# Twenty small copies per layer of a two-block transformer kernel, from VectorE to ScalarE

## The chip, the cores and the metric

The kernel runs on one core of a Trainium2 chip. What counts is the device time of one execution in microseconds (us). Its engines are TensorE (PE, with its weight loads listed as PEld), VectorE (DVE), ScalarE (ACT), GpSimd (POOL) and SyncE (SP), which issues nearly all DMAs. Each engine takes its instructions in the order in which they stand in its own queue and waits on semaphores for the others.

## The reference, cut to what matters

The reference chains two blocks of two layers each on a sequence of 512 tokens of width 1024, all in float32. The change lies in the second block, in the attention of each of its two layers:

```
def nsa_mixer(q, k_all, v_all, gates, q_norm, k_norm, cmp_pe, cmp_w1, cmp_w2):
    q = rope(rms_norm(q, q_norm), pos)                  # 8 heads of 64
    k_s = rope(rms_norm(k_all[:, :, 1], k_norm[1]), pos)  # 2 groups
    k_w = rope(rms_norm(k_all[:, :, 2], k_norm[2]), pos)
    k_cmp = rope(rms_norm(compress(k_all[:, :, 0], ...), k_norm[0]), cmp_end)  # 31 keys
    v_cmp = compress(v_all[:, :, 0], ...)
    o_cmp = softmax(q k_cmp) v_cmp;  o_s = softmax(q k_s) v_s;  o_w = softmax(q k_w) v_w
    return g[..., 0] * o_cmp + g[..., 1] * o_s + g[..., 2] * o_w
```

Around it stand a projection of the layer's input (pooling inputs, keys and values, queries, gates), a pooling mixer, an output projection and a feed-forward network.

## The kernel before

**Arithmetic.** A float32 product is made of three matmuls in the type fp32r: a value is split into a high half (a cast to fp32r) and a low half (the value minus the high half), and high times high, high times low and low times high are summed. Weights come in units of 128x1024 by DMA (`wraw`) and are cut by `unit`: the high half `wH` by a cast on ACT (line 452), the low half `wL` by a subtraction on DVE (line 453). Activations are mostly cut by `split`: a cast on ACT (419), a subtraction on DVE (420).

**The stage of the change.** In `block2`, `weave` interleaves four generators: `main2` makes the projections (their accumulators are `acc` and `accn`), `nsa_prep` and then `nsa` the attention, `compressed` the 31 compressed keys, `pool` the pooling mixer. `nsa_prep` takes the four 128-token tiles of the queries, one after the other: sums of squares (588, 590), the root by a power on POOL (578), the rotation (1573 and 1577 on DVE, 1576 on POOL), the high half (1621) and the low half (1622) of a 128x512 tile `qs`, eight transposes on PE by a product with the identity `keep` (415), and two casts on ACT into `qT` (1628). The keys go the same way in four 128x256 tiles (1639 to 1651), with a copy of the high half on POOL (1643). `compressed` ends with the halves of 64x64 compressed keys (1673 to 1675), and eight copies of 32x128 pieces of the compressed values into `vc` (1694).

`nsa` then runs 16 steps, 8 heads by 2 branches. A step is a chain over the engines: scores on PE (tiles `S`), mask, scale and row maximum on DVE (710), the exponential on ACT (711), the division by the sum on POOL (1764) and DVE (1766), transposes on PE (415, tiles `M`), a split (419 on ACT, 420 on DVE), and the product with the values on PE (406, `M<-p,b`). `main2` puts the last matmuls of the pooling projection and the output projection (`accn`, added up on DVE by 1507) between them.

**Order.** The functions write the program in the order of `weave`; then the Tile framework's scheduler, at build time, orders each engine's queue by its own estimate of when each instruction can run. So an instruction moved from one engine to another can change the order of others, far behind it, too.

## Time and profile before

| | |
|---|---|
| median of 3 runs | 2393.4 us (2393.25 to 2394.74) |
| the profiled execution | 2391.33 us, span of its instructions 2389.5 us |
| PE, DVE, ACT, POOL busy | 98%, 69%, 44%, 11% of the span |
| attention stage of layer 1 of block 2 | about 1240 to 1420 us of the span |
| the same of layer 2 | about 1840 to 2010 us |

A row of the page's list of groups gives a line, an engine, an operation, its tiles and count, then the busy time and the mean of one, then how long the engine had been idle just before and what ended that. A row of the timeline gives the start, the duration, and in square brackets the idle time before it. PE's rows overlap each other, as matmuls are pipelined: the distance from start to start is what one costs.

### The profile page before, as it was taken

Reading aid. Unit: us, or ns where it says so; the run is one execution under the profiler, and the core shown is the slowest. Engines: PE = TensorE matmul, PEld = TensorE weight load, DVE = VectorE, ACT = ScalarE, POOL = GpSimd, SP = SyncE. Lnnn points to the kernel's source line nnn. Section 1 sums busy time; section 2 is a strip of 40 time slices with the busy share of each in tenths; the row PEclk is TensorE's granted clock in tenths of the full one; section 3 lists DMA queues with packets and bytes.
Section 4 is the critical chain, followed back from the end, with each engine's and each line's share of the span. In section 5 each row is a group of like instructions: output and inputs, shape, how many; then the busy total and the mean of one; then the engine's idle time right before and its main releaser. Section 6 shows DMA issues by size and latency. Waiting matters only on the chain.

```text
span 2389.5 us, 31476 instructions
## 1 busy us (share of the span) xinstructions
PE 2342.3 (98%) x11684; PEld 1973.3 (83%) x11684; DVE 1640.2 (69%) x3410; ACT 1048.7 (44%) x1930; POOL 264.3 (11%) x254
## 2 busy tenths in 40 slices
PE   8999999999999999999999989999999998999999
PEld 7888888888888888888888778888888876888888
DVE  5679975567588987656579886666647988644342
ACT  6455543434446554343246654332324665433231
POOL 0011010000001001000055310000005531000000
PEclk9999999999999999999999999999999999999999
DMA  5222222245543222225332013555523211223222
GB/s 173 88 80 71 80 80 97 82 156 205 182 159 115 71 80 80 97 88 172 126 102 80 27 37 104 193 194 194 193 97 105 68 35 37 80 94 100 98 93 84
DMA packets 87851, 256.62 MB, mean 107 GB/s; under 512 B 9745, under 2 KB 10769, under 8 KB 87697
## 3 DMA queue, kind: packets, MB, share of 16 engines
q1 hardware_dynamic: 87552, 254.45, 31.9%
q8 instruction: 92, 1.51, 0.3%
q14 instruction: 63, 0.51, 0.1%
q10 hardware_dynamic: 144, 0.15, 0.0%
HBM read 250.37 MB, written 4.19 MB: 107 GB/s over the span
## 4 chain that ended last, share of the span: by engine, by line
PE 93%; DVE 5%; ACT 1%; issue 1%; DMA 0%; POOL 0%; DVEq 0%; ACTq 0%; POOLq 0%
PE acc L406 78%; PE M L406 5%; PE accn L406 4%; PE S L406 3%; PE M L415 3%; DVE p L420 1%; DVE p L710 1%; DVE b L1507 1%; DVE wL L453 1%; ACT p L419 0%; DVE p L1766 0%; ACT p L711 0%; DVE tmp_s L1794 0%; DMA wraw<-wp_in 0%; ACT tmp_s L1792 0%
## 5 line engine op out<-in xcount | busy, mean ns | idle before, releaser
L406 PE MATMUL acc<-h,wH 128*128 128x512 f32 (+2 forms) x2944 | 872.6, 380 | 9.5 <-ACT h L423 7.3
L452 ACT CAST wH<-wraw 128x1024 fp32r<-128x1024 f32 x358 | 375.2, 1051 | 656.8 <-PE acc L406 400.0
L406 PEld LDWEIGHTS acc<-h,wH 128*128 128x128 f32 (+1 forms) x2944 | 537.4, 189 | 106.1 <-ACT h L423 7.3
L453 DVE TENSOR_TENSOR wL<-wraw,wH 128x1024 fp32r<-128x1024 f32 x358 | 437.5, 1223 | 164.9 <-ACT wH L452 156.9
L406 PE MATMUL acc<-h,wL 128*128 128x512 f32 (+1 forms) x1440 | 546.2, 380 | 0.0
L406 PE MATMUL acc<-b,wH 128*128 128x512 f32 (+1 forms) x1696 | 503.9, 374 | 0.0
L406 PEld LDWEIGHTS acc<-b,wH 128*128 128x128 f32 x1696 | 311.8, 189 | 56.3
L406 PEld LDWEIGHTS acc<-h,wL 128*128 128x128 f32 x1440 | 272.7, 190 | 49.6
L406 PE MATMUL acc<-wH,h 128*128 128x512 f32 (+1 forms) x1024 | 310.0, 380 | 0.0
L406 PE MATMUL acc<-b,wL 128*128 128x512 f32 (+1 forms) x784 | 291.5, 372 | 0.0
L406 PEld LDWEIGHTS acc<-wH,h 128*128 128x128 f32 x1024 | 187.2, 188 | 33.7
L406 PE MATMUL acc<-wL,h 128*128 128x512 f32 (+1 forms) x512 | 194.7, 380 | 0.0
L1390 DVE SCALAR_TENSOR_TENSOR b<-acc,keep,b 128x512 f32<-128x512 f32 (+1 forms) x68 | 48.9, 720 | 183.9 <-PE acc L406 183.5
L406 PEld LDWEIGHTS acc<-b,wL 128*128 128x128 f32 x784 | 147.9, 189 | 25.4
L711 ACT ACTIVATE p<-p,nb 128x128 f32<-128x128 f32 x192 | 107.9, 564 | 77.7 <-DVE nb L710 76.7
L1325 DVE SCALAR_TENSOR_TENSOR keep<-keep 128x512 f32<-128x512 f32 x192 | 126.0, 686 | 11.1 <-DMA keep<-w_mod_in 10.9
L578 POOL TENSOR_TENSOR sm_bs<-sm_as,keep 128x4 f32<-128x4 f32 (+1 forms) x48 | 65.7, 1376 | 413.4 <-DVE sm_as L574 374.1
L406 PEld LDWEIGHTS acc<-wL,h 128*128 128x128 f32 x512 | 96.5, 188 | 16.2
L406 PE MATMUL S<-b,b 128*128 128x128 f32 (+3 forms) x480 | 108.9, 338 | 0.1
L710 DVE CUSTOM_DVE_ANT_0 p<-S,keep 128x128 f32<-128x128 f32 x192 | 101.3, 542 | 4.9 <-PE S L406 3.6
L415 PE MATMUL M<-keep,p 128*128 128x128 f32 x608 | 97.4, 275 | 2.7 <-DVE tmp_s L1794 1.0
L406 PE MATMUL M<-p,b 128*128 128x256 f32 (+3 forms) x352 | 81.7, 323 | 10.3 <-DVE p L420 9.0
(294 smaller groups left out, 2898.8 us busy)
## 6 DMA issues: line engine op xcount, KB each, us to landing
wraw<-wp_in SPq DMA_DIRECT2D x364, 512.0 KB, 3.5
keep<-w_mod_in SPq DMA_DIRECT2D x192, 256.0 KB, 3.6
b<-x_in SPq DMA_DIRECT2D x8, 256.0 KB, 6.3
g<-x_in SPq DMA_DIRECT2D x8, 256.0 KB, 4.4
x_spill<-tmp_m SPq DMA_DIRECT2D x8, 256.0 KB, 3.9
g<-x_spill SPq DMA_DIRECT2D x8, 256.0 KB, 3.8
out<-b SPq DMA_DIRECT2D x6, 256.0 KB, 2.0
keep<-parq_in SPq DMA_DIRECT2D x2, 384.0 KB, 6.9
```

The costliest lines, as they stand in the source:

```text
L406: return self.nc.tensor.matmul(out, l, r, start=start, stop=stop)
L415: self.nc.tensor.transpose(out, in_, self.ident[:n, :n])
L420: return self.nc.vector.tensor_sub(l, src, fbits(h))
L452: self.cut_h = nc.scalar.copy(h, raw)
L453: self.cut = nc.vector.tensor_sub(l, raw, fbits(h))
L578: self.pow = nc.gpsimd.tensor_tensor(r[:p, :n], m[:p, :n], self.mhalf[:p, :n], ALU.pow)
L710: nc.vector.tensor_tensor_reduce(p, s, mask, nscale, 3e38, ALU.add, ALU.min, accum_out=nb)
L711: nc.scalar.activation(p, p, AF.Exp, bias=nb, scale=-1.0, accum_out=accum)
L1325: nc.vector.scalar_tensor_tensor(w, w, 1.0, crow[:, T * k:T * k + T], ALU.mult, ALU.mult, accum_out=ms[:, 2 * f + k:2 * f + k + 1])
L1390: nc.vector.scalar_tensor_tensor(x(m)[:, ts], ps[:, ts], mt[:, 40 + m:41 + m], x(m)[:, ts], ALU.mult, ALU.add)
L1507: nc.vector.scalar_tensor_tensor(x(m)[:, ts], ps[:, ts], mt[:, 16 + m:17 + m], x(m)[:, ts], ALU.mult, ALU.add)
```

## The change

Five lines, in `nsa_prep` and `compressed`, say `nc.scalar.copy` in place of `nc.vector.tensor_copy`. Per layer these are 4 casts of 128x512 (queries), 4 casts of 128x256 (keys), a cast and a copy of 64x64 (compressed keys), and 8 copies of 32x128 (compressed values). All else of the text is the same.

```
-            nc.vector.tensor_copy(qs[:, :, 0, :].bitcast(F32R), qr)
+            nc.scalar.copy(qs[:, :, 0, :].bitcast(F32R), qr)
             nc.vector.tensor_sub(qs[:, :, 1, :], qr, qs[:, :, 0, :])
...
-            nc.vector.tensor_copy(ks[:, :, 0, :].bitcast(F32R), kn)
+            nc.scalar.copy(ks[:, :, 0, :].bitcast(F32R), kn)
             nc.vector.tensor_sub(ks[:, :, 1, :], kn, ks[:, :, 0, :])
             nc.gpsimd.tensor_copy(ks[:, :, 2, :], ks[:, :, 0, :])
...
-        nc.vector.tensor_copy(ks[:, 0, :].bitcast(F32R), kc[:, 2, :])
+        nc.scalar.copy(ks[:, 0, :].bitcast(F32R), kc[:, 2, :])
         nc.vector.tensor_sub(ks[:, 1, :], kc[:, 2, :], ks[:, 0, :])
-        nc.vector.tensor_copy(ks[:, 2, :], ks[:, 0, :])
+        nc.scalar.copy(ks[:, 2, :], ks[:, 0, :])
...
-                nc.vector.tensor_copy(vc[32 * h:32 * h + 32, g, h, :], fbits(vs[32 * g:32 * g + 32]).rearrange("p w d -> p (w d)"))
+                nc.scalar.copy(vc[32 * h:32 * h + 32, g, h, :], fbits(vs[32 * g:32 * g + 32]).rearrange("p w d -> p (w d)"))
```

The queues change at more places than these. On ACT, at the queries of layer 1 (`p_2073` and `p_2083` are the tiles `qs` of the first and the second 128 tokens, `tmp_s_2071` and `tmp_s_2081` the rotated queries):

```order
 L588 ACTIVATE tmp_s_2077_10906<-b_2062_10848 128x512
 L1466 COPY b_2062_10848<-acc_2048_10726 128x512
+L1621 CAST p_2073_10881<-tmp_s_2071_10875 128x8x64
 L588 ACTIVATE tmp_s_2094_10973<-b_2062_10848 128x512
 L452 CAST wH_2118_11079<-wraw_11077 128x1024
 L1466 COPY b_2062_10848<-acc_2049_10727 128x512
+L1621 CAST p_2083_10921<-tmp_s_2081_10915 128x8x64
 L588 ACTIVATE tmp_s_2120_11107<-b_2062_10848 128x512
```

Two casts now stand between the squares of later tiles, a weight cast and an eviction of projected queries.

On PE, at the same place (`M_2075` and `M_2076` take the transposes of the first tile of queries, `acc_2085` is a sum of the key and value projection):

```order
 L406 MATMUL acc_2085_10927<-wH_2090_10933,h_1986_10307 128x512
 L406 MATMUL acc_2085_10927<-wH_2090_10933,h_1985_10306 128x512
+L415 MATMUL M_2075_10894<-keep_1_61,p_2073_10881 128x128 x4
+L415 MATMUL M_2076_10900<-keep_1_61,p_2073_10881 128x128 x4
 L406 MATMUL acc_2085_10927<-wL_2091_10934,h_1985_10306 128x512
 L406 MATMUL acc_2085_10927<-wH_2090_10933,h_1986_10307 128x512
```

These eight transposes stood 14 projection matmuls later before.

On PE, at the first scores of the attention (`M_2173` and `M_2174` take transposes of the third tile of keys, `S_2187` and `S_2189` are the first scores of head 0, `accn_2207` a sum of the pooling projection):

```order
+L415 MATMUL M_2173_11335<-keep_1_61,p_2172_11331 128x128
 L406 MATMUL accn_2207_11446<-h_1985_10306,wH_2205_11442 128x512
 L406 MATMUL accn_2207_11446<-h_1986_10307,wH_2205_11442 128x512
-L415 MATMUL M_2173_11335<-keep_1_61,p_2172_11331 128x128 x4
+L406 MATMUL accn_2207_11446<-h_1985_10306,wL_2206_11443 128x512
+L415 MATMUL M_2173_11335<-keep_1_61,p_2172_11331 128x128 x3
 L415 MATMUL M_2174_11341<-keep_1_61,p_2172_11331 128x128 x4
 L406 MATMUL S_2187_11381<-b_2146_11252,b_2065_10864 128x128 x2
-L406 MATMUL accn_2207_11446<-h_1985_10306,wL_2206_11443 128x512
 L406 MATMUL accn_2207_11446<-h_1987_10308,wH_2205_11442 128x512
```

One projection matmul went from behind the first score to ahead of it.

On PE, in the middle of the attention (`S_2364` and `S_2367` are scores of head 3 against the selected keys, `S_2376`, `S_2382` and `S_2390` scores of head 3 against the window's keys, `M_2344` the last product of the pooling mixer):

```order
 L406 MATMUL S_2364_12060<-b_2146_11252,b_2065_10864 128x384 x2
 L406 MATMUL S_2367_12071<-b_2146_11252,b_2065_10864 128x512 x2
-L406 MATMUL S_2376_12105<-b_2147_11253,b_2065_10864 128x128 x2
-L406 MATMUL S_2382_12121<-b_2147_11253,b_2065_10864 128x256 x2
-L406 MATMUL S_2390_12167<-b_2147_11253,b_2065_10864 128x384 x2
 L406 MATMUL M_2344_11973<-tmp_p_2339_11959,b_2199_11425 128x512
 L406 MATMUL M_2346_11986<-p_2327_11917,b_2139_11197 128x512
```

The three scores taken out here now stand further back, one at a time between transposes and products with the values. Layer 2 has the same differences at the same places. SP's queue is the same in both.

## Rows read from the trace of the kernel before

**Rows 1.** The page: busy time by engine, and the chain that ended last.

```profile
PE 2342.3 (98%) x11684; PEld 1973.3 (83%) x11684; DVE 1640.2 (69%) x3410; ACT 1048.7 (44%) x1930; POOL 264.3 (11%) x254
PE 93%; DVE 5%; ACT 1%; issue 1%; DMA 0%; POOL 0%; DVEq 0%; ACTq 0%; POOLq 0%
```

**Rows 2.** Stretch, length, busy us (count) of PE, PEld, DVE, ACT, POOL, clock, DMA.

```profile
1245.00:1300.00 55.00, 55.00 (x288) 46.11 (x287) 49.84 (x128) 30.57 (x71) 32.66 (x35) 1.00 0.29 96
1300.00:1420.00 120.00, 109.15 (x613) 89.30 (x612) 105.89 (x291) 76.94 (x209) 37.37 (x44) 1.00 0.11 36
...
1845.00:1900.00 55.00, 55.00 (x292) 46.24 (x291) 48.60 (x133) 32.39 (x77) 29.08 (x36) 1.00 0.22 70
1900.00:2010.00 110.00, 101.25 (x569) 82.82 (x568) 99.35 (x272) 71.40 (x195) 33.47 (x39) 1.00 0.10 34
```

**Rows 3.** PE's waits, 1300 to 1420: total us, times, longest.

```profile
PE M L406 <- DVE p L420: 4.5, 9, 1.0
PE accn L406 <- ACT b L419: 2.0, 1, 2.0
```

**Rows 4.** Groups of VectorE by shape, 1240 to 1300: busy us, mean ns.

```profile
L1621 DVE CAST p<-tmp_s 128x512 fp32r<-128x512 f32 x4 | 2.1, 533 | 0.1
...
L1694 DVE CAST b<-tmp_c 32x128 fp32r<-32x128 f32 x8 | 1.7, 218 | 0.2
...
L1673 DVE CAST tmp_c<-tmp_c 64x64 fp32r<-64x64 f32 x1 | 1.7, 1651 | 0.0
...
L1641 DVE CAST p<-tmp_s 128x256 fp32r<-128x256 f32 x4 | 1.4, 351 | 0.0
```

**Rows 5.** Groups of ScalarE by shape, 1230 to 1300: casts out of SBUF.

```profile
L419 ACT CAST tmp_p<-tmp_p 128x512 fp32r<-128x512 f32 x1 | 0.6, 623 | 0.0
...
L419 ACT CAST tmp_c<-tmp_c 64x64 fp32r<-64x64 f32 x1 | 0.2, 244 | 1.1 <-POOL sm_bc L578 1.1
```

**Rows 6.** Timeline of VectorE at the queries of layer 1: start, us, instruction.

```profile
1242.78 1.12 DVE L1577 TENSOR_TENSOR tmp_s<-tmp_s,tmp_s 128x512 f32<-128x512 f32 x1
...
1244.49 0.41 DVE L1621 CAST p<-tmp_s 128x512 fp32r<-128x512 f32 x1
1244.82 0.68 DVE L1577 TENSOR_TENSOR tmp_s<-tmp_s,tmp_s 128x512 f32<-128x512 f32 x1
...
1246.78 1.13 DVE L1622 TENSOR_TENSOR p<-tmp_s,p 128x512 f32<-128x512 f32 x1
...
1248.18 1.21 DVE L453 TENSOR_TENSOR wL<-wraw,wH 128x1024 fp32r<-128x1024 f32 x1
...
1251.26 0.68 DVE L1622 TENSOR_TENSOR p<-tmp_s,p 128x512 f32<-128x512 f32 x1
```

**Rows 7.** Timeline of ScalarE there: the weight cast behind the first moved cast.

```profile
1243.63 1.05 ACT L452 CAST wH<-wraw 128x1024 fp32r<-128x1024 f32 x1 [1.20 <-DMA wraw<-wp_in]
```

**Rows 8.** The chain that ended last, 1240 to 1300: start, us, what.

```profile
1248.77 0.87 PE M L415 x8
1249.64 2.74 PE acc L406 x12
```

**Rows 9.** Timeline of GpSimd at the same place.

```profile
1245.66 1.70 POOL L1576 TENSOR_TENSOR tmp_s<-b,keep 128x256 f32<-128x256 f32 x2
...
1251.22 1.82 POOL L1576 TENSOR_TENSOR tmp_s<-b,keep 128x256 f32<-128x256 f32 x2
```

**Rows 10.** Timeline of VectorE at the first scores of layer 1 and layer 2.

```profile
1290.63 0.62 DVE L710 CUSTOM_DVE_ANT_0 p<-S,keep 128x384 f32<-128x384 f32 x1 [1.66 <-PE S L406]
...
1884.23 0.62 DVE L710 CUSTOM_DVE_ANT_0 p<-S,keep 128x384 f32<-128x384 f32 x1 [1.98 <-PE S L406]
```

**Rows 11.** Timeline of TensorE in mid-attention, then VectorE a little later.

```profile
1330.74 2.97 PE L406 MATMUL S<-b,b 128*128 128x128 f32 x14
1335.53 0.50 PE L406 MATMUL M<-tmp_p,b 128*128 128x512 f32 x1 [1.83 <-ACT tmp_p L419]
...
1348.05 0.75 DVE L1507 SCALAR_TENSOR_TENSOR b<-accn,keep,b 128x512 f32<-128x512 f32 x1 [1.97 <-PE accn L406]
```

## The prediction

> **What bounds the kernel now.** I read the page's busy times and its chain first: TensorE is busy 98% of the span, and 93% of the chain that ended last is its own work [rows 1]. So a move between VectorE and ScalarE can change the time only where TensorE waits. Next, the table of stretches [rows 2]. From 1245 to 1300 us, where all twenty copies of layer 1 lie, TensorE is busy 55.00 of 55.00 us; layer 2 reads the same from 1845 to 1900. VectorE has 49.84 of these 55 us, ScalarE 30.57. In the attention behind it, from 1300 to 1420, TensorE has 109.15 of 120 us, so 10.85 us are idle, and in layer 2 (1900 to 2010) 110 - 101.25 = 8.75 us. These 19.6 us are all that the attention of both layers could give back. Third, TensorE's waits in that stretch [rows 3]: the largest is for the low half of the transposed probabilities on VectorE (4.5 us in 9 waits), next 2.0 us for a ScalarE cast. VectorE's load, 105.89 of 120 us, is the nearest rival of TensorE there, and none of the moved copies lies in it.
>
> **What leaves VectorE.** Per layer, from the groups by shape [rows 4]: four casts of 128x512 for 2.1 us, four of 128x256 for 1.4 us, one of 64x64 for 1.65 us, eight of 32x128 for 1.7 us, and the 64x64 copy, counted like one of the eight, 0.2 us. The sum is 7.0 us, and 49.84 would become about 43.
>
> **What comes to ScalarE.** The nearest rows are casts from SBUF to SBUF: 623 ns for 512 columns, 244 ns for 64 [rows 5], so 0.846 ns a column; an estimate from these is 406 ns for 256 and 298 ns for 128. Four by 623, four by 406, two by 244 and eight by 298 make 2.49 + 1.62 + 0.49 + 2.38 = 7.0 us. ScalarE goes from 30.57 to about 37.6 of 55 us. What hides this is its 24 us of idle time; without it the 7.0 us would stand once per layer before the attention.
>
> **The waits that are added.** A cast that followed its input on VectorE now takes a turn to ScalarE and back. I follow the first tile of queries. Its rotated values were ready when the 1.12 us addition ended, at 1243.90 [rows 6]. On ScalarE the cast takes 0.62 us, to about 1244.5. What is queued behind it there (squares of a later tile, then a weight cast) slips: that weight cast started at 1243.63 [rows 7] and would start at about 1243.90 + 0.62 + 0.6 = 1245.1. The subtraction that needs it ran only at 1248.18 [rows 6], more than two microseconds after the new end of 1246.2. So that costs nothing. On VectorE the subtraction 1622 now waits for ScalarE, with sums and rotations of later tiles behind it; the order puts the second tile's addition ahead of it as a filler: 1244.49 + 0.68 = 1245.17, later than the cast's end, so VectorE should not stand still.
>
> TensorE is another matter. The eight transposes of that tile started at 1248.77, and the order lifts them past 14 matmuls of 2.74/12 = 0.228 us [rows 8], 3.2 us, so to 1245.6. Their input is ready when the low half is: 1245.17 plus 0.68 to 1.13 us, the two durations that line 1622 shows [rows 6], so 1245.85 to 1246.30. TensorE waits 0.25 to 0.7 us where it did not wait before; I take 0.5. The ends for the range are 0 (the transposes come just in time) and 1.2 (the hand-over to ScalarE finds the engine busy with one more 0.6 us operation).
>
> The long subtraction started at 1246.78, while GpSimd was at work from 1245.66 to 1247.36; but the short one, at 1251.26, had GpSimd beside it too, from 1251.22 [rows 9]. So the rows do not settle which length the new one has, and 0.5 stays the middle.
>
> The Trainium skill (GPSIMD Engine Reference, Specifications) says that GpSimd shares its SBUF interfaces with VectorE and contends with VectorE instructions that have two SBUF inputs, as this subtraction has. By that rule the new subtraction, at 1245.2 beside GpSimd's work, would take 1.13 us and TensorE's wait be 0.7, the sum 0.4 us higher over both layers; this trace agrees at the one place and not at the other.
>
> The later tiles have more room. Their transposes move by 0 to 1.4 us of TensorE's work, counted in the order by columns at that pace, while VectorE reaches their subtractions earlier by what has left it. The compressed keys' chain gets shorter (0.24 in place of 1.65 us for its cast). The keys' copy on GpSimd now waits for ScalarE instead of VectorE and still has the freed time as cover. I set all these at nothing; without the cover each would cost one hand-over of the size above, 0.5 us.
>
> **Where the 7 us on VectorE go.** At the first scores VectorE already waits: it stood idle 1.66 us before 1290.63 in layer 1 and 1.98 us before 1884.23 in layer 2, both times for scores from TensorE [rows 10]. TensorE has no gap before that, and the order puts the first scores one 0.23 us matmul later, not earlier. What VectorE saves ahead of this point lengthens its wait there. So I put the gain in the attention at 0; it is bounded by 7.0 us per layer, and a loss is not excluded, because the order of the scores changes behind this point.
>
> **The sum.** The profiled execution took 2391.33 us (its span 2389.5 us and 1.8 us around it). Add 2 x 0.5 = 1.0 us for the first transposes: 2392.3. The profiled execution was 2.07 us below the median of the three timed ones, 2393.4, so the forecast for the median is 2394.4 us. Its own bounds, from 0 to 1.2 us per layer and some 3 us either way for the attention's changed order (two of its waits, each of up to 2 us and less than its whole), are 2390 to 2399.
>
> **Rivals.**
>
> *The relief reaches TensorE.* The attention's waits are mostly for VectorE [rows 3], and work that VectorE does early (pooling sums, weight subtractions, the softmax of the compressed branch) could leave it freer at 1300 to 1345. Also, TensorE stood 1.83 us in mid-attention for a split of the pooling mixer behind a batch of 14 score matmuls [rows 11], and the new order takes three score tiles out of that batch. For this speak 10.85 and 8.75 us of idle TensorE; against it that VectorE had caught up with TensorE at 1290.63. If half of the 7 us per layer arrives: 2393.4 - 7 = 2386.4 us. If all: 2379.4.
>
> *The new order of the scores starves VectorE, and the time gets longer.* In the second half of the attention the order puts window scores of head 3 behind up to 6 us of other TensorE work, and other heads' scores similarly. VectorE's mask step needs scores, and it stood 1.97 us before 1348.05 while TensorE ran projection matmuls [rows 11]. If late scores make such a pause of VectorE twice more per layer, the chain mask, exponential, transpose, split, product comes later by 2 x 1.97 = 3.9 us, and TensorE, with its filler spent, waits for it: 2394.4 + 7.9 = 2402.3 us. It decides once a pause is longer than the filler that stands between two steps. For it speaks that VectorE is at 88% there, so that a pause is hard to make up; against it that the scores are moved behind useful work and not behind a wait.
>
> *The change does not do what it says.* The two casts of the queries stand in ScalarE's queue, so this has no chance of its own.
>
> **How the numbers follow.** About 0.2% of the time, 4.8 us, is what a measurement of this kernel can tell from no change. The forecast, within 2388.6 to 2398.2, has a chance of 0.55: TensorE's fixed work ahead of the attention and the wait at its entry both hold the effect near zero. The relief that arrives has 0.2. The late scores have 0.25; they come above the relief because both layers have the same order, so a bad spot counts twice, and the saved time has a visible place where it is lost. Faster is then 0.2, same 0.55, slower 0.25. The range reaches to the middle of either rival: 2385.5 to 2402.5; what it leaves out is the full relief and more than two lost pauses per layer, about 0.15.
>
> **What would show it.** Right: VectorE's busy time from 1245 to 1300 falls to about 43 us and ScalarE's rises to about 37; a short wait of TensorE appears at the first transposes of the queries, at about 1245.6; VectorE's wait before its scores near 1290 grows by several us; TensorE's idle time from 1300 to 1420 stays within 3 us of 10.85. Wrong: idle time there of 7 us or less (the relief arrived), or of 15 us or more, with VectorE waiting for `S` in mid-attention (the late scores). Wrong, too, if ScalarE's weight casts run late enough that TensorE waits for `wH` or `wL` in the projections.

## The result, and the profile after

The changed kernel takes 2409.23 us (median of six runs, 2407.79 to 2410.52), the kernel before 2392.02 us in the runs beside it. The ratio is 1.0071 (95% interval 1.0060 to 1.0082): slower by 17 us, where the forecast was no change. The profiled execution is the one of 2407.79 us, its span 2406.0 us.

The page after, busy time and the chain that ended last, against [rows 1]:

```profile
PE 2352.1 (98%) x11684; PEld 1980.4 (82%) x11684; DVE 1632.0 (68%) x3374; ACT 1060.6 (44%) x1966; POOL 265.7 (11%) x254
PE 92%; DVE 5%; ACT 2%; DMA 1%; issue 1%; POOL 0%; DVEq 0%; ACTq 0%; POOLq 0%
```

TensorE has the same 11684 records and is busy 9.8 us longer with them. That is the first sign: the same work took it more time. VectorE has 36 instructions fewer and ScalarE 36 more, so 18 copies per layer moved; the title and the prediction say twenty, but the list in the section on the change comes to 4 + 4 + 2 + 8 = 18, too. The stretches of [rows 2]:

```profile
1245.00:1300.00 55.00, 55.00 (x288) 46.06 (x286) 43.52 (x107) 36.45 (x90) 31.08 (x33) 1.00 0.26 79
1300.00:1420.00 120.00, 108.72 (x596) 89.78 (x595) 104.31 (x288) 74.03 (x202) 37.52 (x44) 0.97 0.11 36
1845.00:1900.00 55.00, 54.68 (x287) 45.53 (x286) 43.20 (x106) 35.99 (x88) 31.53 (x35) 1.00 0.27 89
1900.00:2010.00 110.00, 101.65 (x562) 84.73 (x560) 99.77 (x272) 70.67 (x191) 36.25 (x43) 0.98 0.12 39
```

VectorE lost and ScalarE gained what was forecast, and TensorE's idle time from 1300 to 1420 hardly moved (11.28 us against 10.85). What moved in the second row is the count, 596 matmuls where there were 613, and the clock, 0.97 where it was 1.00. A stretch cut by time hides this. Cut instead from one place in TensorE's queue to another (from its 6914th to its 7172nd matmul in layer 1, from its 9813th to its 10102nd in layer 2), the end of the attention reads as follows (first the kernel before, layer 1 and layer 2, then the changed kernel; columns as in [rows 2]):

```profile
1395.20:1450.00 54.80, 44.16 (x259) 38.91 (x258) 43.08 (x104) 27.21 (x67) 7.11 (x8) 0.88 0.12 39
1985.02:2045.10 60.08, 49.53 (x291) 43.82 (x291) 48.47 (x115) 30.33 (x72) 8.55 (x10) 0.89 0.11 36
```

```profile
1393.01:1456.86 63.85, 50.91 (x261) 42.42 (x259) 43.65 (x105) 29.24 (x70) 7.41 (x8) 0.79 0.08 25
1991.17:2061.62 70.45, 56.85 (x292) 47.54 (x291) 49.95 (x124) 33.52 (x81) 9.28 (x10) 0.81 0.09 30
```

These two stretches got 9.05 and 10.37 us longer: more than the whole loss, because the profiled execution of the changed kernel was 3.5 us ahead of that of the kernel before when it came to the queries, up to where the two queues are the same. (The matmuls inside are not quite the same ones: in the changed kernel they have 512 columns more in layer 1 and 2688 fewer in layer 2. At 0.228 us for 512 columns, [rows 8], that is an estimated 0.2 us more work and 1.2 us less.) I call these stretches the **tail** below: the last three of the 16 steps, the output projection's last matmuls, and the start of the feed-forward network.

In the tail two things grew. TensorE's idle time (length less busy) went from 10.6 to 12.9 us, and in layer 2 from 10.6 to 13.6. And TensorE ran longer at 1.2 GHz instead of 2.4: a mean clock of 0.88 over 54.80 us is 2 x 0.12 x 54.80 = 13 us at half speed, 0.79 over 63.85 us is 27 us; the same in layer 2. The Trainium skill (TensorE: Matmul & The Clock Gate, Terms) puts the price of throttled time at that time by the share of clock pulses withheld, here one half. Half of 13.6 us more would be 6.8 us, and 6.8 + 2.3 = 9.1 us would be the whole of layer 1's loss, 6.8 + 3.0 = 9.8 of 10.4 in layer 2. This sum comes out by chance. Cut once more, at the attention's last product, it no longer does. I call the part of the tail up to that product the **steps** (before, layer 1 and 2, then changed):

```profile
1395.20:1417.27 22.07, 19.38 (x118) 15.99 (x117) 18.65 (x51) 12.47 (x35) 5.53 (x6) 1.00 0.15 49
1985.02:2010.82 25.80, 23.09 (x138) 19.21 (x137) 22.37 (x58) 14.32 (x39) 6.97 (x8) 1.00 0.13 42
```

```profile
1393.01:1424.12 31.11, 25.77 (x120) 19.36 (x118) 19.50 (x52) 14.54 (x38) 5.82 (x6) 0.83 0.06 18
1991.17:2025.90 34.73, 28.71 (x138) 21.56 (x137) 23.53 (x66) 17.59 (x48) 7.69 (x8) 0.88 0.10 30
```

The steps got 9.0 and 8.9 us longer. Behind them, up to the end of the tail, layer 1 takes 32.7 us in both kernels, though its time at 1.2 GHz rose there too (a clock of 0.79 before and 0.75 after). What the half clock costs in the steps is measured below; it is far less than half.

TensorE's timeline shows what happens there. Layer 1, before (start, us, instruction, idle time before it and what ended that):

```profile
1401.08 0.49 PE L415 MATMUL M<-keep,p 128*128 128x128 f32 x3
...
1405.04 0.62 PE L406 MATMUL S<-b,b 128*128 128x512 f32 x2
1405.49 0.62 PE L406 MATMUL accn<-b,wH 128*128 128x512 f32 x2
...
1409.84 1.15 PE L415 MATMUL M<-keep,p 128*128 128x128 f32 x9
1412.00 1.21 PE L406 MATMUL M<-p,b 128*128 128x512 f32 x5 [1.01 <-DVE p L420]
...
1417.27 0.67 PE L406 MATMUL M<-b,b 128*128 128x512 f32 x2
1419.98 1.12 PE L406 MATMUL accn<-b,wH 128*128 128x512 f32 x2 [2.04 <-ACT b L419]
```

and after:

```profile
1400.74 0.63 PE L406 MATMUL accn<-b,wH 128*128 128x512 f32 x2
...
1401.90 0.61 PE L415 MATMUL M<-keep,p 128*128 128x128 f32 x4
1403.25 0.49 PE L406 MATMUL M<-p,b 128*128 128x512 f32 x1 [0.73 <-ACT p L419]
1404.57 0.55 PE L415 MATMUL M<-keep,p 128*128 128x128 f32 x3 [0.83 <-DVE p L420]
1404.87 0.48 PE L406 MATMUL M<-p,b 128*128 128x512 f32 x1
1405.68 0.44 PE L406 MATMUL M<-p,b 128*128 128x384 f32 x1 [0.33 <-ACT p L419]
...
1407.67 0.58 PE L406 MATMUL M<-p,b 128*128 128x256 f32 x1 [0.55 <-ACT p L419]
...
1409.23 2.15 PE L415 MATMUL M<-keep,p 128*128 128x128 f32 x9
...
1412.24 1.05 PE L406 MATMUL S<-b,b 128*128 128x512 f32 x2
...
1414.38 0.63 PE L406 MATMUL accn<-b,wH 128*128 128x512 f32 x2
...
1424.12 1.17 PE L406 MATMUL M<-b,b 128*128 128x512 f32 x2
1427.32 1.22 PE L406 MATMUL accn<-b,wH 128*128 128x512 f32 x2 [2.04 <-ACT b L419]
```

Before, the ready projection matmuls (`accn`, `acc`) stand between the steps, and the last score of the attention (`S`, 128x512) starts at 1405.04. After, most of that projection work stands ahead of the third-last step (the `accn` row at 1400.74 belongs to it; nine more matmuls follow from 1414.38 on, ahead of the last step), and the third-last and the last step run bare: four transposes, a wait for the split, one product, a wait, three transposes, and so on. I call that **lockstep**. The last score comes at 1412.24. The rows also show the clock: nine transposes took 1.15 us and take 2.15, the two score matmuls 0.62 and now 1.05. The granted clock of three stretches after:

```profile
1396.00:1406.50 10.50, 8.46 (x47) 6.60 (x46) 8.98 (x22) 5.47 (x14) 4.00 (x4) 1.00 0.17 52
1406.50:1413.30 6.80, 6.11 (x23) 4.75 (x21) 3.42 (x11) 4.03 (x12) 0.00 (x0) 0.50 0.00 1
1420.20:1430.40 10.20, 7.59 (x20) 5.26 (x21) 2.76 (x6) 2.07 (x5) 0.00 (x0) 0.50 0.00 0
```

Before, TensorE was at full clock until 1420 [rows 2].

### The profile page after: what moved, and what is told of

Read it like the earlier page. It is cut to its first block, busy times and chain, and to the rows that moved or that the text cites. A ratio compares the mean times of both kernels' runs of the same rounds, so it can differ in the third digit from the quotient of the medians.

```text
span 2406.0 us, 31474 instructions
## 1 busy us (share of the span) xinstructions
PE 2352.1 (98%) x11684; PEld 1980.4 (82%) x11684; DVE 1632.0 (68%) x3374; ACT 1060.6 (44%) x1966; POOL 265.7 (11%) x254
## 4 chain that ended last, share of the span: by engine, by line
PE 92%; DVE 5%; ACT 2%; DMA 1%; issue 1%; POOL 0%; DVEq 0%; ACTq 0%; POOLq 0%
PE acc L406 75%; PE M L406 5%; PE accn L406 4%; PE S L406 4%; PE M L415 3%; DVE wL L453 1%; DMA wraw<-wp_in 1%; DVE p L420 1%; DVE p L710 1%; DVE p L1766 0%; ACT p L419 0%; DVE b L1507 0%; ACT wH L452 0%; ACT p L711 0%; DVE b L1449 0%
## 5 line engine op out<-in xcount | busy, mean ns | idle before, releaser
L1325 DVE SCALAR_TENSOR_TENSOR keep<-keep 128x512 f32<-128x512 f32 x192 | 126.0, 686 | 11.2 <-DMA keep<-w_mod_in 10.8
L415 PE MATMUL M<-keep,p 128*128 128x128 f32 x608 | 103.9, 284 | 8.9 <-POOL p L1764 2.8
L406 PE MATMUL M<-p,b 128*128 128x256 f32 (+3 forms) x352 | 89.4, 338 | 12.2 <-ACT p L419 5.6
```

The costliest lines, as they stand in the source:

```text
L406: return self.nc.tensor.matmul(out, l, r, start=start, stop=stop)
L415: self.nc.tensor.transpose(out, in_, self.ident[:n, :n])
L1325: nc.vector.scalar_tensor_tensor(w, w, 1.0, crow[:, T * k:T * k + T], ALU.mult, ALU.mult, accum_out=ms[:, 2 * f + k:2 * f + k + 1])
```

## Experiments

Three theories stand at the start. A: the new order at the attention's end costs the time. B: each copy moved to ScalarE costs, where it stands or behind it. C: as A, but the price is TensorE's half clock more than its waits. D (lockstep) and E (filler and last score together) came later.

All kernels are timed against the kernel before on the same chip (its median lay between 2391.1 and 2392.2 us). The table gives the tail of layer 1 / layer 2, cut at the same places of TensorE's queue as above, from one row per layer of each profile: length, idle time of TensorE (length less busy), and us at 1.2 GHz (2 x (1 - clock) x length). The last two columns give the length of the steps alone and the us at 1.2 GHz in them. In the four kernels with the order of before in the tail (before, e2, e3, e4) the steps agree within 0.1 us.

| kernel | median us | ratio, 95% interval | tail, us | idle | at 1.2 GHz | steps, us | at 1.2 GHz in them |
|---|---|---|---|---|---|---|---|
| before | 2392.0 | 1 | 54.8 / 60.1 | 10.6 / 10.6 | 13 / 13 | 22.1 / 25.8 | 0 / 0 |
| changed | 2409.2 | 1.0060 to 1.0082 | 63.9 / 70.5 | 12.9 / 13.6 | 27 / 27 | 31.1 / 34.7 | 11 / 8 |
| e1 queries only | 2409.4 | 1.0070 to 1.0100 | 65.1 / 70.0 | 13.1 / 14.2 | 27 / 24 | 31.1 / 34.2 | 9 / 5 |
| e2 keys only | 2388.5 | 0.9978 to 0.9996 | 54.7 / 58.9 | 10.5 / 10.7 | 13 / 11 | 22.0 / 25.8 | 0 / 0 |
| e3 compressed only | 2391.5 | 0.9993 to 1.0011 | 53.6 / 59.7 | 10.6 / 10.5 | 11 / 13 | 22.1 / 25.8 | 0 / 0 |
| e4 new casts, old order | 2391.0 | 0.9989 to 1.0006 | 55.3 / 58.8 | 10.5 / 10.4 | 13 / 11 | 22.1 / 25.8 | 0 / 0 |
| e5 old casts, new order | 2414.5 | 1.0081 to 1.0111 | 64.4 / 70.9 | 12.6 / 13.2 | 27 / 31 | 30.7 / 35.0 | 9 / 11 |
| e6 new order mended | 2403.9 | 1.0039 to 1.0064 | 60.1 / 66.9 | 12.1 / 13.1 | 17 / 20 | 27.6 / 31.2 | 3 / 1 |
| e7 last score late | 2391.5 | 0.9990 to 1.0008 | 55.1 / 60.3 | 11.3 / 11.2 | 13 / 13 | 24.0 / 27.7 | 3 / 3 |
| e9 last 99 new | 2416.7 | 1.0095 to 1.0122 | 68.5 / 69.8 | 14.6 / 15.0 | 30 / 21 | 34.0 / 34.9 | 12 / 3 |
| e10 filler first | 2392.9 | 0.9997 to 1.0014 | 54.9 / 59.6 | 12.0 / 11.9 | 10 / 11 | 23.4 / 27.1 | 0 / 0 |
| e13 lockstep | 2400.6 | 1.0021 to 1.0046 | 58.3 / 63.0 | 12.4 / 12.3 | 14 / 14 | 25.3 / 29.0 | 0 / 0 |
| e14 changed, no lockstep | 2411.7 | 1.0074 to 1.0100 | 65.3 / 70.0 | 16.9 / 17.5 | 27 / 24 | 33.9 / 37.1 | 16 / 12 |
| e15 filler first, score late | 2397.3 | 1.0015 to 1.0032 | 58.6 / 63.7 | 12.6 / 12.4 | 18 / 17 | 26.0 / 29.7 | 4 / 4 |
| e16 lockstep, filler first | 2397.4 | 1.0019 to 1.0038 | 57.5 / 62.8 | 12.6 / 13.1 | 10 / 10 | 25.9 / 30.0 | 0 / 0 |

### Which of the casts, and is it the casts or the order?

The first three kernels move only some of the copies, each by the lines of the diff that concern it. e1:

```
-            nc.vector.tensor_copy(qs[:, :, 0, :].bitcast(F32R), qr)
+            nc.scalar.copy(qs[:, :, 0, :].bitcast(F32R), qr)
```

> Only the four query casts of each layer (line 1621) go to ScalarE. TensorE's queue in the last 20 us of each attention is then word for word the one of the full change: the last score of the attention (tile S_2577 in layer 1) stands behind the transposes of the step before it, and three groups of output-projection matmuls that filled the end stand earlier. Theory A (the order at the attention's end costs the time): the full loss, 2409 us, +14 to +18 us against before, and nearly all of it behind 1395 us and behind 1985 us. Theory B (each cast moved to ScalarE costs there, in the queries' stage and behind it): the four query casts are 2.5 of the 6.7 us of copies moved per layer, so about 6 us, 2398 us, spread over the stage. Theory C (TensorE's half clock at the end is the price): as A, with some 27 us per layer at 1.2 GHz, where before has 13.7.

e2 has the same at the keys (line 1641):

> Only the four key casts of each layer (line 1641) go to ScalarE. TensorE's queue changes between the keys and the middle of the attention, and from there to the attention's end it is again that of before. Theory A: no loss at the end, 2392 us, within 3 us of before. Theory B: 1.6 of the 6.7 us of copies moved per layer, so about 4 us, 2396 us. Theory C: as A, with some 13.7 us per layer at 1.2 GHz, as before.

e3 has it at lines 1673, 1675 and 1694:

> Only the cast and the copy of the compressed keys and the eight copies of compressed values of each layer (lines 1673, 1675, 1694) go to ScalarE. TensorE's queue is word for word that of before, and VectorE's differs by the ten instructions alone. Theory A: 2392 us, within 1.5 us of before. Theory B: 2.5 of the 6.7 us of copies moved per layer, so about 6 us, 2398 us. If this gains (VectorE 2.3 us per layer shorter), the rival of the prediction in which the relief reaches TensorE is alive: down to 2388 us.

Measured: the queries alone give the whole loss, the keys alone a gain of 2.6 us, the compressed keys and values nothing. The loss does not go by the load moved (2.5 us of casts lose 18 us, another 2.9 us nothing). It goes with TensorE's queue at the tail, which is that of the changed kernel in e1 and that of before in e2 and e3.

For e4 and e5 a table holds TensorE's queue, matmul by matmul, in the order of the other kernel: 3952 matmuls, from the first transposes of the queries in layer 1 to behind the attention of layer 2, where the two queues differ. The edit, shortened:

```
+    for a, b in zip(PINS, PINS[1:]):      # names of the matmuls, in the wanted order
+        tc.add_manual_dep(ins[b], a, mybir.DependencyInfo(NoSync, DATA), reason="pin")
```

> All moved copies on ScalarE as in the full change, but TensorE's queue is held, matmul by matmul, in the order of the kernel before (edges of order alone, which add no wait for a result). Theory A: the loss is gone, 2390 to 2394 us; what is left against before is the price or gain of the copies on ScalarE by themselves. Theory B: the loss stays, 2409 us. Theory C: as A, with no more than some 14 us per layer at 1.2 GHz.

> No copy is moved: all casts stay on VectorE as before, but TensorE's queue is held, matmul by matmul, in the order of the changed kernel (edges of order alone). Theory A (the order is the whole loss): 2407 to 2411 us. Theory B (ScalarE's copies have a share in it): clearly less, down to 2391 us. Theory C (half clock): as A, with over 50 us at 1.2 GHz in the two layers.

All copies on ScalarE under the old order cost nothing, and the new order without a single moved copy costs 23 us, more than the change itself. So **the casts are harmless and the order is the loss**. Under the new order the moved copies seem to help (2414.5 us without, 2409.2 with them), though the two intervals touch. The tail of e5 reads like that of the changed kernel (table). One thing stays unseparated: the scheduler orders the other engines' queues to suit the held one, so that where TensorE's queue is changed, VectorE's and ScalarE's follow (in the tail of e9, too). "The order" here is TensorE's with what the scheduler makes of the rest; no run changes the others alone.

### What in the order?

From here every kernel holds TensorE's whole queue in the way of e4, and its edit is a change of that queue, the same in both layers. My theory was the late last score and the spent filler. e6 mends both, as far as it could, in the changed kernel's queue (names of layer 1; `M_2570` takes the transposes of the second-last step, `M_2579` its last one):

```
-acc_2609 x3, acc_2610 x3, accn_2595 x3
 M_2544 ... M_2553            transposes of the third-last step, with its products
+S_2577 x2                    the last score
 M_2570, M_2573, M_2576       transposes of the second-last step
-S_2577 x2
+acc_2609 x3, acc_2610 x3, accn_2595 x3
 M_2579
```

> The changed kernel with its own order, but for 11 matmuls in each layer: the last score (tile S_2577 in layer 1, two matmuls) goes 12 matmuls ahead, before the transposes of the step before it, and nine matmuls of the output projection, which stood ahead of that step's transposes, go behind it, where the last step's chain runs. Theory A with the late last score and the spent filler as the cause: at least half of the loss comes back, 2395 to 2402 us, the clock falls less. If the cause lies further ahead in the order (the stretch of heads 5 and 6): 2407 to 2411 us.

e7 makes only the last score late, in the queue of before (behind six matmuls of `accn_2590`, nine of `acc` and seven products).

> The kernel before with one move in each layer: the two matmuls of the last score go 22 matmuls (some 4 us) further back, behind the last product of head 7's first branch; all else of TensorE's queue stays. Theory A: the last step's chain of mask, exponential, division and transposes starts later, with less projection work behind it: 3 to 6 us per layer, 2397 to 2403 us, with more time at 1.2 GHz. If the place of the filler alone matters and not that of the last score: within 2 us of before, 2391 us.

e6 gave back 5 of 17 us, less than expected, and e7 lost nothing as a whole: its tail is 0.3 us longer. But its steps are 1.9 us longer in both layers (23.96 and 27.74 us), with 3 us at 1.2 GHz in them, and what stands behind them is 1.5 and 1.7 us shorter, with 10 us at 1.2 GHz instead of 14. So **the late last score, which is so plain in the timeline, is a fifth of the change's loss in the steps, and not the cause by itself**; why it came back behind is not told by these runs. e9 asks whether the tail is enough: the queue of before, except for the last 99 matmuls ahead of the attention's last product. e10 puts 18 ready matmuls (`accn_2589`, `accn_2590`, three each of `acc_2609` and `acc_2610`) ahead of the third-last step's transposes.

> The kernel before, with all casts where they were and its own order on TensorE, but for the last 99 matmuls ahead of the last product of each attention, which stand as in the changed kernel. Theory A, narrowed (the loss lies in how the last three steps and the last output-projection matmuls are mixed): 2405 to 2412 us. If the order further ahead (heads 0 to 6) has a share: 2394 to 2402 us.

> The kernel before with one change in each attention: 18 ready matmuls of the output projection (two whole sums accn of six, and three of each of two sums acc; some 3.4 us) go ahead of the transposes of the third-last step; the scores and the steps keep their order among themselves. Theory A' (the loss comes from filler that is spent before the last chains, so that they run bare): 3 to 8 us per layer, 2397 to 2407 us, with more idle and more half clock behind 1400 us. If only filler and late last score together cost: within 3 us of before.

The 99 matmuls alone give 26 us, more than the whole change and as much as the new order without the moved copies (e5, 23 us; the intervals overlap). So the order further ahead has no share that shows. Filler first alone gives 1.7 us, within the measurement; in the steps it is 1.3 us in each layer. Next came the lockstep: e13 puts it into the queue of before, e14 takes it out of the changed one; e15 joins the moves of e10 and e7, e16 those of e13 and e10. The edit of e13 at the third-last step:

```
-M_2544 x4, ..., M_2547 x3, ..., M_2550 x2, ..., M_2553      transposes, early, among scores
-M_2535 <- p_2542 x5 ...                                       products, behind them
+M_2544 x4, M_2535 x1, M_2547 x3, M_2535 x2, M_2550 x2, M_2553, ...
```

> The kernel before, where in each attention the transposes of the third-last and of the last step go right ahead of the products that need them, tile by tile (four transposes, one product, three transposes, two products and so on), as they stand in the changed kernel; the filler and the last score stay. Theory D (lockstep: a product stands right behind its own transposes, and TensorE waits for the split between them): the larger part of the loss, 2398 to 2412 us, with waits of 0.3 to 0.9 us between transposes and products. Theory E (spent filler and late last score together): within 3 us of before.

> The changed kernel, where in each attention all ten transposes of the third-last and of the last step go ahead of the first product that needs them; the filler stays early and the last score late. Theory D: 4 to 8 us per layer come back, 2393 to 2401 us. Theory E: within 3 us of the changed kernel, 2406 to 2412 us.

> The kernel before with both single moves at once: 18 output-projection matmuls ahead of the third-last step's transposes, and the last score behind the transposes of the step before it. Theory E: 2403 to 2415 us. Theory D: 2392 to 2397 us, hardly more than either move by itself.

> The kernel before with two moves at once: the lockstep of transposes and products (8.4 us by itself) and the 18 output-projection matmuls ahead of the third-last step's transposes (1.7 us by itself). If the moves add: 2400 to 2404 us. If each costs more where the other has taken the cover away: 2405 to 2416 us, the loss of the last 99 matmuls' whole order.

Lockstep alone is the largest single part, 8 us, and 3.2 us of the steps in each layer. The clock has no share in these 3.2 us: it read 1.00 throughout (e13, layer 1).

```profile
1397.04:1422.32 25.28, 20.61 (x119) 16.28 (x117) 19.46 (x51) 12.83 (x35) 5.35 (x6) 1.00 0.14 43
```

Idle time is 2.0 us more than before, busy time 1.2 us more. A matmul that stands alone between two waits is listed with its whole length, 0.49 us, where two in a row take 0.62, so that waiting lengthens the busy time, too. But taking the lockstep out of the changed kernel gives nothing back, against theory D: its waits of 0.3 to 0.8 us became fewer and longer ones (1.2 to 2.0 us, 16.9 us idle in the tail instead of 12.9). As I read it, that is because no other work is left to stand between. Theory E fails as well: filler first with the late score costs 5 us, not 11 or more.

In the steps the moves come near to adding. Singly they cost 3.2 (lockstep), 1.9 (late score) and 1.3 us (filler first) in layer 1; e15, filler first with late score, costs 3.9, where 3.2 would be the sum, and e16, lockstep with filler first, 3.8, where 4.5 would be. In the totals this is hard to see: what stands behind the steps took from 31.2 to 33.2 us in layer 1, with 10 or 14 us at 1.2 GHz, in kernels that have the same matmuls there in the same order, and the interval of e16 overlaps that of e13. The three moves come to 6.4 of the 9.0 us by which the change lengthens the steps.

### Is the half clock a price of its own?

e8 adds idle matmuls, six per layer, in two waits of the kernel before: two in the 2.04 us at 1417.9, four in the 4.59 us ahead of the feed-forward network's sums. The edit, shortened:

```
+[self.mm(j, self.ident, self.mcaus, True, True) for j in [self.psum("S")] for _ in range(6)]
```

> The kernel before with six idle matmuls added per layer (128x512 of the identity by the mask, into a tile that nobody reads; 5.5 us of TensorE if they run at full clock): two in the wait of 2.04 us behind the last product of the attention, four in the wait of 4.59 us for the sums of squares ahead of the feed-forward network. Theory C (the half clock behind a wait is itself a price): the 10.2 us at 1.2 GHz behind that wait vanish in both layers, 4 to 5 us are won per layer, 2381 to 2384 us. If only the waits themselves count: 2391 us, or up to 4 us more where a fill is longer than its wait.

It takes 2387.5 us, ratio 0.9985 (0.9976 to 0.9994). The fill and the wait that is left of the 4.59 us, then the tails of both layers:

```profile
1427.99 3.59 PE L406 MATMUL S<-keep 128*128 128x512 f32 x8
1432.83 0.35 PE L406 MATMUL M<-keep 128*128 128x1 f32 x2 [1.25 <-DVE keep L657]
...
```

```profile
1394.65:1446.53 51.88, 45.57 (x271) 37.64 (x270) 42.67 (x104) 27.05 (x66) 7.12 (x8) 0.97 0.13 41
1981.52:2038.54 57.02, 50.67 (x303) 42.23 (x303) 47.84 (x114) 29.95 (x72) 8.57 (x10) 0.97 0.12 38
```

Both tails are 3 us shorter (in the fastest of eleven executions; by the medians the kernel gained 4.2 us, some 2 per layer), and the time at 1.2 GHz fell from 13 us to 3. No wait of the real work is gone, so this is the clock alone: yes, it has a price, but 3.0 us for 10 us, not the 4 to 5 that I expected. It came in two parts. Between the two waits TensorE has work of its own; there the same matmuls, before and with the fill, read:

```profile
1419.98:1430.22 10.24, 10.24 (x54) 8.96 (x54) 7.83 (x14) 3.75 (x7) 0.00 (x0) 0.83 0.01 2
```

```profile
1419.45:1428.15 8.70, 8.70 (x55) 7.94 (x56) 7.66 (x14) 3.75 (x7) 0.00 (x0) 1.00 0.01 2
```

3.4 us less at half clock made them 1.5 us shorter, near the half that the Trainium skill's rule cited above gives. Behind the second wait, 6.8 us less won 1.4: part of that stretch was waiting for the norm's chain on VectorE and GpSimd (the 4.59 us wait, and one of 1.22 us behind it), which a faster TensorE cannot shorten. Over both, the rule would have made it 5 us; this run differs.

In the steps the price can be read from three kernels that have the changed kernel's queue there: e1 and e5 beside the changed kernel itself. Layer 2, e1 and then e5 (changed: 34.73 us, 6.02 idle, clock 0.88):

```profile
1992.07:2026.27 34.20, 27.54 (x138) 20.04 (x137) 23.51 (x66) 17.56 (x48) 7.68 (x8) 0.93 0.10 30
```

```profile
2000.29:2035.30 35.01, 29.44 (x138) 22.09 (x137) 23.56 (x66) 17.59 (x48) 7.69 (x8) 0.84 0.09 30
```

From 5 us at 1.2 GHz in e1 over 8 to 11 in e5, the steps get only 0.8 us longer, because TensorE's idle time falls from 6.66 over 6.02 to 5.57 us: where TensorE waits for chains over ScalarE and VectorE, at full clock it waits longer. By that ratio (an estimate) the 8 us of the changed kernel are worth 1 us of the 8.9. So theory C fails in the steps. The half clock comes with the loss; it is not the larger part of its price. A fill was not tried in the steps of the changed kernel.

### Can it be had better?

e11 has the key casts alone with the fill of e8; e12 also holds twelve `acc` matmuls back for the 2.04 us wait, with one half-width idle matmul in place of two.

> Only the key casts on ScalarE, TensorE in that kernel's own order, and the six idle matmuls per layer in the two waits at the attention's end. If the two gains add (2.6 us from the keys alone and 4.2 us from the filled waits): 2384 to 2386 us. If the keys' gain was chance: 2387 to 2388 us.

> As the one with the key casts and filled waits, but the wait of 2.04 us behind the attention's last product is filled with twelve matmuls of the output projection that stood 10 to 60 places ahead of it (1.4 us), and one idle matmul of half width. Theory A' (filler is worth most where nothing else can run): 1 to 3 us better than the same kernel without, 2381 to 2385 us. If the last chains need that filler more: equal or up to 4 us worse.

They take 2387.8 us (ratio 0.9974 to 0.9992) and 2387.1 us (0.9975 to 0.9992). Both beat the kernel before, by 0.17%, but no more than e8 alone: either the two gains do not add or, as the expectation has it for this result, the keys' gain was chance. The held filler gave nothing that can be measured.

e17 and e18 leave the order to the scheduler again, with all casts on ScalarE and one number changed.

```
-RATE3 = 10.0
+RATE3 = 14.0
```

> The changed kernel, all copies on ScalarE, with one number more: RATE3, by which the attention's steps are written ahead of the projection's, 14 in place of 10. The scheduler then builds a tail with the last score 68 matmuls ahead of the attention's last product (38 in the changed kernel, 69 in before), and ten projection matmuls among the last 20. Theory A (the order is the whole loss): 2386 to 2394 us. If the moved casts cost by themselves: 2405 us or more.

> As the one with 14, with RATE3 at 20: the last score stands 81 matmuls ahead of the attention's last product, the transposes of the third-last step 114 to 96 (102 to 84 in before, 68 to 57 in the changed kernel), and nine projection matmuls are among the last 20. Theory A: 2386 to 2394 us. If the moved casts cost by themselves: 2405 us or more.

e17 takes 2391.0 us (0.9992 to 1.0010): the loss is gone with all copies on ScalarE and a queue that nobody held. e18 takes 2407.6 us (1.0056 to 1.0083), against my expectation, with the number that theory B gave and yet with a good tail (56.7 us in layer 1, though by its own order that holds somewhat other matmuls). Much of its loss lies elsewhere, at a wait from 1300 to 1340 (us in total, times, longest) that the kernel before does not have and that layer 2 repeats:

```profile
PE M L415 <- DVE tmp_c L1725: 4.6, 1, 4.6
```

There TensorE's queue has the transposes of the compressed branch ahead of their turn. In e17 the casts cost nothing. That they have no part in e18 is argued from the place of this wait and from e4, not shown: no run has that rate with the casts on VectorE. It looks as if each new order had its own bad spot, or none.

## Why the prediction was wrong

**What bounds the kernel** was read rightly, with one error in it: "19.6 us idle are all that the attention could give back" bounds a gain. I let it stand for the size of a loss, too. A loss is not bounded by idle time, and of the 19.4 us that came in the two tails only 5.3 are idle time.

**What leaves VectorE and comes to ScalarE** was right: 49.84 to 43.52 us (forecast 43) and 30.57 to 36.45 (forecast 37). The moved copies by shape on ScalarE, priced at 623, 298, 406 and 244 ns:

```profile
L1621 ACT CAST p<-tmp_s 128x512 fp32r<-128x512 f32 x4 | 2.5, 619 | 5.6 <-DVE tmp_s L1577 5.6
L1694 ACT CAST b<-tmp_c 32x128 fp32r<-32x128 f32 x8 | 2.4, 298 | 1.2 <-POOL b L1689 1.1
L1641 ACT CAST p<-tmp_s 128x256 fp32r<-128x256 f32 x4 | 1.6, 407 | 2.6 <-DVE tmp_s L1639 2.4
L1673 ACT CAST tmp_c<-tmp_c 64x64 fp32r<-64x64 f32 x1 | 0.2, 247 | 2.8 <-DVE tmp_c L1671 2.8
```

e4 shows that they cost nothing where the order is kept.

**The first transposes** did wait, for the reason given, but 2.40 us in layer 1 and 0.3 in layer 2 (54.68 of 55 us busy) where I took 0.5 each:

```profile
1244.49 1.06 PE L415 MATMUL M<-keep,p 128*128 128x128 f32 x8 [2.40 <-DVE p L1622]
```

TensorE was there at 1242.09, 3.5 us earlier than the 1245.6 that I had worked out from the old trace, since this execution was that much ahead when it came to the queries; VectorE was 1.4 us ahead. So the term was 2.7 us instead of 1.0 over both layers in this execution, but most of the 2.40 is a lead given back and no cost of the change; layer 2, without such a lead against VectorE, has the size that I forecast. The subtraction ahead of it took 0.68 us (at 1243.67, with a GpSimd record of 128x8 elements at 1242.64 lasting 1.64 us beside it), the shorter of the two durations. The Trainium skill (GPSIMD Engine Reference, Specifications) would have it slowed by GpSimd's work on the shared SBUF interfaces; this row does not show that.

**VectorE's longer wait for the first scores** did not come: 1.25 us before the mask at 1289.77, 1.66 before, and 1.33 us in layer 2, 1.98 before [rows 10]. Where its saved time went is not shown. The second half of the attention, ahead of the tail, did get shorter, by 1.4 us in layer 1 and 0.8 in layer 2 (cut where both queues have done the same work). Layer 1, before, changed, e4 (all copies moved, old order) and e5 (none moved, new order):

```profile
1349.95:1396.42 46.47, 44.74 (x252) 37.42 (x251) 42.61 (x119) 29.38 (x82) 10.96 (x13) 1.00 0.12 40
```

```profile
1349.32:1394.35 45.03, 44.17 (x252) 37.47 (x251) 41.58 (x115) 27.56 (x78) 10.58 (x12) 1.00 0.15 47
```

```profile
1348.96:1395.46 46.50, 44.76 (x252) 37.41 (x251) 42.63 (x119) 29.34 (x82) 10.93 (x13) 1.00 0.13 39
```

```profile
1354.39:1399.72 45.33, 44.46 (x251) 37.44 (x250) 41.55 (x115) 27.56 (x78) 10.60 (x12) 1.00 0.16 47
```

So even this gain goes with the new order and not with VectorE's lighter load: the rival "the relief reaches TensorE" had no share that shows.

**The step that failed is the changed order of the attention**, set at nothing with "some 3 us either way", two waits of up to 2 us each. It was 19.4 us in the two tails (some 17 with the gain ahead of them). It was mis-sized in two ways. I looked at the order at the first scores and in the middle, not at the end, and, as I read it, the end is the one place where nothing follows that could make up for a late step. And I priced a late step by its wait alone: of the 9.0 and 8.9 us by which the steps got longer, idle time is 2.7 and 3.3 us. The rest counts as busy: matmuls that stand alone between two waits, and matmuls at half clock. In [rows 2] the clock reads 1.00 up to 1420, so I took full speed for granted; but the kernel before is itself at half clock behind 1420, and the changed kernel is so from 1406.5 on. That part is worth about 1 us per layer (estimated above), where half of the 8 to 11 us at 1.2 GHz would be 4 to 5.

**The rival "late scores starve VectorE"** had the right sign and the right picture (scores behind projection work, the filler spent), at the wrong place and price: 2402.3 us by 3.9 us of waits per layer in mid-attention. No such pause came there (VectorE's longest wait for scores between 1300 and 1420 is 0.98 us), and TensorE's idle time in the tails grew by 2.3 and 3.0 us. Its mark, idle time of 15 us or more from 1300 to 1420, could not have shown it: that stretch ends where the loss is at its height, and half clock counts as busy.

**The wait for weights** did not come; nor did "the change doesn't do what it says".

What stays open: what makes up the rest of the loss. The three moves that were tried come to 6.4 of the 9.0 us in the steps of layer 1; all 99 matmuls together cost 26 us. And why the clock falls in one thin stretch and not in another (the steps of e13, e15 and e16 have 4.6 to 5.3 us of idle time, and only those of e15 have time at half clock) is not told by these runs.

## What to carry to other kernels

Moving an instruction between engines, under a scheduler that orders every queue by its own estimates, is two changes: the instruction's own price, which the rows gave to within 2% and which came to nothing here, and a new order everywhere behind it, which cost 17 us; hold the old order (e4) and the old assignment (e5) apart before judging either. Read the new order first at the end of each stage, where filler is spent and no later work covers a late chain, and cut the stages by the same work instead of the same time, and finely: the tail as a whole hid that all of layer 1's loss lay ahead of its last product. And look at the granted clock beside the idle time, but do not price it by halves: where TensorE has work of its own 3.4 us at half clock cost 1.5, where it waits for other engines 6 us more cost 0.8.

## What was not expected of the hardware

TensorE fell to 1.2 GHz at 1406.5 us although none of its waits in the 5 us before was longer than 0.83 us; the row of 1396.00 to 1406.50 has it busy 8.46 of 10.50 us at full clock. Filling 5.5 us of waits per layer with matmuls that do nothing kept the clock up and made the tail 3 us shorter.

A 64x64 cast that took 1651 ns on VectorE [rows 4] takes 247 ns on ScalarE, while the 128x512 cast went the other way, from 533 to 619 ns. But the 1651 ns are not what a cast of this shape costs VectorE. The trace of the kernel before, VectorE and then GpSimd:

```profile
1259.69 1.65 DVE L1673 CAST tmp_c<-tmp_c 64x64 fp32r<-64x64 f32 x1
...
1261.52 0.18 DVE L1675 COPY tmp_c<-tmp_c 64x64 f32<-64x64 f32 x1
```

```profile
1258.60 1.81 POOL L1679 MEMSET b<- 128x2048 f32 x1
1260.35 0.95 POOL L1689 MEMSET b<- 128x1024 f32 x1
```

GpSimd fills two tiles beside it, and the cast ends at 1261.34, just behind the second fill's end at 1261.30; in layer 2, and in e5 in both layers, it also ends 0.05 us behind that fill. The copy of the same shape, with no fill beside it, takes 0.18 us. So the cast was held up by the fills, as far as the times tell; no run moves them.
